# Prompt attention on one Trainium2 core: the last 16 keys of a query block turned onto higher partitions, and the value products of two units run together

## The chip, the cores and the metric

The kernel runs on one NeuronCore of a Trainium2 chip. A core has five engines that run side by side, each through its own instructions in order: TensorE (PE in the profile; its weight loads are listed apart as PEld), VectorE (DVE), ScalarE (ACT), GpSimd (POOL) and SyncE (SP, which here only issues DMAs). They meet through semaphores. The metric is the device time of one execution in microseconds: 2818.92 us, the median of three runs (2814.28 to 2822.15).

## The reference

One inference step of a two-layer decoder for a prompt of 1024 tokens (with 16 meta tokens ahead of it) and for eight short decode requests. The part that matters here is the attention of the prompt: 16 heads of 64, 1040 keys, causal, with a per-key log-forget sum `c` added to the scores.

```python
def one_block(args):
    qi, ci, pi = args
    s = jnp.einsum('bqhd,bkhd->bhqk', qi, k, preferred_element_type=f32)
    s = s + ci.astype(f32).transpose(0, 2, 1)[..., None] - ckT[:, :, None, :]
    s = jnp.where(pos_k[None, :] <= pi[:, None], s, -jnp.inf)
    p = jax.nn.softmax(s, axis=-1)
    return jnp.einsum('bhqk,bkhd->bqhd', p.astype(v.dtype), v)
```

The result is multiplied by a sigmoid gate, which the kernel has stored as `og2D`.

## The kernel before

The prompt attention is one stage, `attend_prompt` (L2707 on). It goes through 8 pairs of heads `hp` (two heads, `z` = 0 and 1, on partitions 0 to 63 and 64 to 127), and within a pair through four groups of two query blocks, in the order `QG = (0, 3, 1, 2)`. Query block `qb` = 2g+u+1 sees 16 + 128·qb keys, so there are 2g+1 or 2g+2 full tiles of 128 keys, and 16 keys more at the end. Those last 16 keys are the subject of the change; only the last 32 columns of queries of the block are taken for them.

**Scores** (`scores`, L2814). For each block the keys are cut into pieces (`KSPLIT`, 14 pieces for a pair). A piece is six matmuls (L2841): two heads by three products of high and low parts, into two PSUM tiles `sp`. There are three `sp` buffers in all. VectorE (L2845) adds the forget row `ncb` (or, for the diagonal 128 keys, `nd`, which GpSimd makes from `ncb` at L2811), takes the running maximum, and so frees the buffer. ScalarE takes the exponential (L2868).

**Units** (`units`, L2871). Two key tiles make a unit; a group has g+1 of them, and the last one, with `tail`, has one or two tiles and the 16 keys. `turn` turns the probabilities on TensorE: a 64 x 128 piece of the row `s` is the stationary operand and the identity the moving one (L2895), into the PSUM tile `tp` (two buffers). The tail turns its 16 keys by four ordinary float32 matmuls with 16 columns of `s` as weights (L2899; the profile counts two per float32 matmul), out to partitions 0 to 15. ScalarE copies `tp` to `th` (L2903) and the 16 rows to `tail` (L2905), a 128 x 128 tile that is zero elsewhere. `prod` multiplies with the values (L2928, L2932) and, for the 16 keys, `tail` with tile 2g+1+u of `vr`, whose first 16 rows are these keys (L2936); before that it spreads the reciprocal sums with four transposes (L2923). Products land in the PSUM tile `op`, of which there is one. VectorE then does three multiplications (L2939, L2942), and GpSimd splits the result (L2945, L2946).

**Order.** TensorE, VectorE, ScalarE and GpSimd take the order in which the code is written. The loop at the end of `attend_prompt` does for each unit: score pieces that are due (`ahead`), `turn`, exponentials, score pieces, and then `prod` of the unit before (`late`). The order on SP is not written; the framework places the DMAs there. SP issues the loads of the stage: for a pair, queries and keys `qh`, `kh`, `kl`, `ql` (L2760), the forget rows `ncb` (L2761), the values `vr` (L2767) with the 16 last keys apart into a ninth tile that GpSimd clears first (L2768, L2769), and the gates `og` (L2773). At the start of the stage the matmuls of the last gate tiles (`og`, L193 to L195) stand between the score pieces. The stage ahead of it is the attention of the decode requests, whose meta-token part ends in L2678, L2685 and L2691.

Of the kernel before, what the change touches and what calls it, by code (L numbers as in the profile page):

```python
# [8 lines left out]
F32 = mybir.dt.float32  # L9
# [8 lines left out]
P = 128  # L18
# [4 lines left out]
NM = 16  # L23
# [2683 lines left out]
def attend_prompt(self, ys):  # L2707
# [3 lines left out]
    with self.pool("ap", bufs=1) as sp, self.pool("ap2", bufs=2) as s2, self.pool("app", bufs=2, space=PSUM) as pp:  # L2711
# [41 lines left out]
        def place_c(hp):  # L2753
            return s2.tile([P, 2, NP], F32, name=f"ncb_{hp}", tag=f"ncb{hp % 2}", bufs=1)
# [116 lines left out]
        def units(hp, g):  # L2871
# [7 lines left out]
            out = []  # L2879
            for j0 in range(0, nf, 2):  # L2880
# [3 lines left out]
                def turn(j0=j0, tail=tail, hold=hold):  # L2884
                    pt = pp.tile([P, 2, 8, 64], F32, name=f"tp{hp}_{g}_{j0}", tag="tp")
                    th = s2.tile([P, 2, 2, 256], F32, name=f"th{hp}_{g}_{j0}", tag="th", bufs=3)
                    hold["th"] = th
# [4 lines left out]
                    for y, (z, u, j) in enumerate(ts):  # L2892
                        for h in range(2):
                            r = slice(h * 64, h * 64 + 64)
                            nc.tensor.transpose(pt[:, h, y], ss[z, u][r, j * P : j * P + P], self.ident[r, r])  # L2895
                    if tail:
                        for z in range(2):
                            for u in range(2):
                                nc.tensor.matmul(pt[:NM, 1, 6 + z, u * 32 : u * 32 + 32],  # L2899
                                                 ss[z, u][64:, (nf + u) * P : (nf + u) * P + NM],  # L2900
                                                 self.ident[64:, 96:], start=True, stop=True)
                    n = len(ts)
                    nc.scalar.copy(th.rearrange("p x z (u h q) -> p h (x z u) q", h=2, q=64)[:, :, :n], pt[:, :, :n])  # L2903
                    if tail:
                        nc.scalar.copy(tw[:NM], pt[:NM, 1, 6:].rearrange("p a q -> p (a q)"))  # L2905
                        hold["r"] = firstm.pop("r") if "r" in firstm else s2.tile([P, 2, 2], F32, name=f"r{hp}_{g}",
                                                                                  tag="r", bufs=4)
                        nc.vector.reciprocal(hold["r"], sm)
                        rx = hold["rx"] = firstm.pop("rx") if "rx" in firstm else s2.tile(
                            [P, 2, 2, DH], F32, name=f"rx{hp}_{g}", tag="rx")  # L2910
                        nc.gpsimd.tensor_copy(rx, hold["r"].unsqueeze(3).broadcast_to([P, 2, 2, DH]))

                def prod(j0=j0, tail=tail, hold=hold):
                    th = hold["th"]
                    mm = nc.tensor.matmul
                    if tail:


                        hold["rs"] = [hold["pt"][:, 0, 6:], po[:, 256:384].rearrange("p (u q) -> p u q", u=2)]
                        for u in range(2):  # L2920
                            for h, x in enumerate(hold["rs"]):
                                r = slice(h * 64, h * 64 + 64)
                                mm(x[:, u], hold["rx"][r, u].rearrange("p z d -> p (z d)"), self.ident[r, r],  # L2923
                                   start=(h == 0 or j0 == 0), stop=True, is_transpose=True, skip_group_check=True)
                    ds = [slice(z * 64, z * 64 + 64) for z in range(2)]
# [7 lines left out]
                    for u in range(2):  # L2933
                        for z in range(2):
                            c = (2 * z + u) * 32
                            mm(po[ds[z], u * P + 96 : u * P + P], vr[:, nf + u, ds[z]], tw[:, c : c + 32],  # L2936
                               start=False, stop=(u == 1))
# [9 lines left out]

                out.append((turn, prod))
            return out
# [12 lines left out]
        with tc.manual_schedule(engines={E.PE, E.DVE, E.Activation, E.Pool}):  # L2962
# [48 lines left out]
            late()  # L3011

# [33 lines left out]
```

## Time and profile before

| | |
|---|---|
| median of 3 runs | 2818.92 us |
| the profiled execution's own time (its span) | 2818.5 us |
| prompt attention, first score to last product | 1728.9 to about 1981 us |
| one pair of heads in the settled part | about 28.9 us (the piece of 400 columns after the first product run starts at 1818.63 and again at 1847.53) |
| busy in 1820 to 1880: PE, DVE, ACT, POOL | 56.78, 43.35, 45.56, 30.83 of 60 us |

How to read it: the profile is one execution. Its timeline lists an engine's instructions by start and duration, equal ones that follow each other as one row with their count, and in brackets the idle time before a row and what ended it. Two starts that follow each other tell how long the engine was held, which for matmuls is a better measure than the duration, since matmuls overlap. Semaphore waits are put down to the engine whose signal came last.

### The profile page before, as it was taken

The page shows a single profiled execution, that of the slowest core. Times are in us where ns is not written, and L with a number is a line of the kernel's source. Part 1 is how long each engine was busy: PE and PEld are TensorE (multiplying, and loading weights), DVE is VectorE, ACT ScalarE, POOL GpSimd, SP SyncE. Part 2 cuts the span into 40 slices and gives each one's busy share as a digit, 9 for nine tenths or more (in the row PEclk, how much of TensorE's full clock was granted, in tenths as well). Part 3 has the DMA queues.
Part 4 walks back from the last instruction along what each step waited for, and adds up shares of the span by engine and source line. Part 5 has one row for each costly group of instructions (what it writes and reads, how often), then busy time and mean ns, then how long its engine had stood idle before and what let it go on. Part 6 is the DMA issues. An engine that isn't in the chain of part 4 may idle for free. (4 is left out here: it accounts for less than half of the span.)

```text
span 2818.5 us, 60631 instructions
## 1 busy us (share of the span) xinstructions
PE 2762.3 (98%) x23543; PEld 2650.7 (94%) x23543; DVE 1798.8 (64%) x4025; ACT 1177.1 (42%) x2299; POOL 856.1 (30%) x1348
## 2 busy tenths in 40 slices
PE   9999989999999999999999999999999999999998
PEld 8998879999999999999999887677999999999998
DVE  5633566888887655662455444776388888766656
ACT  5432553422223334443444455777343223323345
POOL 3142333223223232124452202444313223323111
PEclk9999999999999999999999999999999999999999
DMA  7666555355564375544443775432524655527556
GB/s 213 174 188 170 151 164 193 108 152 158 173 178 137 120 246 171 192 145 163 145 173 123 264 293 193 161 128 87 157 87 126 177 176 163 162 91 236 179 195 215
DMA packets 432420, 474.05 MB, mean 168 GB/s; under 512 B 37015, under 2 KB 358291, under 8 KB 431107
## 3 DMA queue, kind: packets, MB, share of 16 engines
q1 hardware_dynamic: 380562, 320.52, 36.9%
q0 software_dynamic: 44928, 143.44, 15.5%
q10 hardware_dynamic: 6640, 6.21, 0.7%
q8 instruction: 185, 3.03, 0.5%
q14 instruction: 105, 0.85, 0.1%
HBM read 322.84 MB, written 147.21 MB: 167 GB/s over the span
## 5 line engine op out<-in xcount | busy, mean ns | idle before, releaser
L1614 PE MATMUL m<-xh,slot 128*128 128x276 f32 x2752 | 541.0, 290 | 1.8 <-ACT fs L1643 1.8
L1614 PEld LDWEIGHTS m<-xh,slot 128*128 128x128 f32 x2752 | 440.1, 188 | 3.6 <-ACT fs L1643 2.2
L1614 PE MATMUL m<-xl,slot 128*128 128x276 f32 x1376 | 397.3, 289 | 0.0
L1614 PEld LDWEIGHTS m<-xl,slot 128*128 128x128 f32 x1376 | 259.0, 188 | 0.0
L193 PE MATMUL tmps<-slot,xh 128*128 128x256 f32 (+2 forms) x864 | 243.1, 281 | 0.0
L195 PE MATMUL tmps<-slot,xl 128*128 128x256 f32 (+2 forms) x864 | 240.6, 278 | 0.0
L194 PE MATMUL tmps<-slot,xh 128*128 128x256 f32 (+2 forms) x864 | 240.5, 278 | 0.0
L272 DVE TENSOR_TENSOR slot<-slot,slot 128x1024 fp32r<-128x1024 f32 x124 | 162.9, 1314 | 60.1 <-ACT slot L271 58.7
L271 ACT CAST slot<-slot 128x1024 fp32r<-128x1024 f32 x124 | 129.5, 1045 | 142.6 <-PE m L1614 111.7
L194 PEld LDWEIGHTS tmps<-slot,xh 128*128 128x128 f32 (+1 forms) x864 | 159.1, 184 | 0.1
L195 PEld LDWEIGHTS tmps<-slot,xl 128*128 128x128 f32 (+1 forms) x864 | 158.6, 184 | 0.0
L193 PEld LDWEIGHTS tmps<-slot,xh 128*128 128x128 f32 (+1 forms) x864 | 158.4, 183 | 0.2
L193 PE MATMUL mmA<-xh,whi 128*128 128x384 f32 (+1 forms) x384 | 135.2, 352 | 0.1
L195 PE MATMUL mmA<-xh,wlo 128*128 128x384 f32 (+1 forms) x384 | 128.2, 334 | 0.0
L194 PE MATMUL mmA<-xl,whi 128*128 128x384 f32 (+1 forms) x384 | 128.1, 334 | 0.0
L272 DVE TENSOR_TENSOR slot<-vA,slot 128x1024 fp32r<-128x1024 f32 (+1 forms) x59 | 82.2, 1396 | 32.7 <-ACT slot L271 31.5
L272 DVE TENSOR_TENSOR slot<-Ht,slot 128x1024 fp32r<-128x1024 f32 (+1 forms) x59 | 81.4, 1382 | 32.2 <-ACT slot L271 31.1
L271 ACT CAST slot<-Ht 128x1024 fp32r<-128x1024 f32 (+1 forms) x59 | 61.0, 1036 | 96.8 <-PE m L1614 92.9
L271 ACT CAST slot<-vA 128x1024 fp32r<-128x1024 f32 (+1 forms) x59 | 60.8, 1035 | 95.5 <-PE m L1614 88.5
L1718 DVE TENSOR_TENSOR ws<-ws 128x128 f32<-128x128 f32 x264 | 93.8, 355 | 8.9
L2868 ACT ACTIVATE s<-s,nb 128x272 f32<-128x272 f32 (+7 forms) x126 | 98.8, 786 | 0.0
L2903 ACT COPY th<-tp 128x768 f32<-128x768 f32 (+1 forms) x80 | 73.6, 920 | 55.9 <-PE tp L2895 32.8
(809 smaller groups left out, 8688.7 us busy)
## 6 DMA issues: line engine op xcount, KB each, us to landing
ws<-in_w_down SPq DMA_DIRECT2D x176, 128.0 KB, 2.7
sD<-ws SPq DMA_DIRECT2D x176, 128.0 KB, 2.1
slot<-sD SPq DMA_DIRECT2D x40, 512.0 KB, 4.0
slot<-in_w_gate_up SPq DMA_DIRECT2D x36, 512.0 KB, 4.1
kp<-in_cache_k SPq DMA_DIRECT2D x32, 512.0 KB, 7.1
vp<-in_cache_v SPq DMA_DIRECT2D x32, 512.0 KB, 5.5
vA<-in_w_gate_up SPq DMA_DIRECT2D x26, 512.0 KB, 3.9
Ht<-in_w_gate_up SPq DMA_DIRECT2D x26, 512.0 KB, 3.9
```

Of the source, the lines that this page charges most:

```text
L193: mm(ps, sh, mh, start=first, stop=False)
L194: mm(ps, sh, ml, start=False, stop=False)
L195: mm(ps, sl, mh, start=False, stop=last)
L271: self.nc.scalar.copy(hi, src)
L272: self.nc.vector.tensor_tensor(out=lo, in0=src, in1=hi.bitcast(F32), op=ALU.subtract)
L1614: nc.tensor.matmul(u.ps[h, b], w[p][:, k], x[q][:, k], start=first and k == i == 0, stop=k == 3 and i == 2, skip_group_check=True)
L1718: tt(out=o, in0=a, in1=b, op=ALU.subtract)
L2868: nc.scalar.activation(ss[z, u], ss[z, u], AF.Exp, bias=nb[:, z : z + 1], accum_out=sm[:, u, z : z + 1])
L2903: nc.scalar.copy(th.rearrange("p x z (u h q) -> p h (x z u) q", h=2, q=64)[:, :, :n], pt[:, :, :n])
```

## The change

The last 16 keys are turned by weights of 80 columns (even pairs) or 112 columns (odd pairs) that end at these keys, so that they come out on partitions 64 to 79 or 96 to 111; columns ahead of them land on lower partitions of `tp` and are not read. Their values no longer lie in the first rows of the next `vr` tile but in a tile `vt` of their own, on the same partitions, one slot for each query block. `vt` is one tile for the whole stage, cleared once and loaded pair by pair. There are four `tail` tiles in place of two. The spread of the reciprocals is taken out of `prod` into `spread`. The products are held until two units wait, or until the last that waits is a group's tail; then `flush` runs the spreads and after them the products. A fourth `th` tile, `thx`, joins the three, and the four are used in turn.

```diff
-            nc.gpsimd.memset(vr[:, 8, :], 0.0)
-            e.dma_start(vr[:NM, 8, :], self.vD[8 * P :, cs])
+            e.dma_start(vt[at_tail(hp), :, :], self.vD[NM:, cs].rearrange("(j p) d -> p j d", p=P)[P - NM :])
...
+        vt = sp.tile([P, 8, P], F32, name="vt")
+        thx = sp.tile([P, 2, 2, 256], F32, name="thx")
+        tails += [sp.tile([P, P], F32, name=f"tail{x}") for x in (2, 3)]
+        for x in (vt, *tails[2:]):
+            nc.gpsimd.memset(x, 0.0)
+        at_tail = lambda hp: slice(64 + 32 * (hp % 2), 64 + 32 * (hp % 2) + NM)
+        ths = []
+
+        def place_t(nm):
+            if len(ths) < 4:
+                ths.append(thx if len(ths) == 3 else s2.tile([P, 2, 2, 256], F32, name=nm, tag="th", bufs=3))
+                return ths[-1]
+            ths.append(ths.pop(0))
+            return ths[-1]
...
-            tw = tails[QG.index(g) & 1]
+            tw = tails[2 * (hp % 2) + (QG.index(g) & 1)]
...
                     if tail:
+                        m = at_tail(hp).stop
                         for z in range(2):
                             for u in range(2):
-                                nc.tensor.matmul(pt[:NM, 1, 6 + z, u * 32 : u * 32 + 32],
-                                                 ss[z, u][64:, (nf + u) * P : (nf + u) * P + NM],
+                                e = (nf + u) * P + NM
+                                nc.tensor.matmul(pt[:m, 1, 6 + z, u * 32 : u * 32 + 32], ss[z, u][64:, e - m : e],
                                                  self.ident[64:, 96:], start=True, stop=True)
...
-                        nc.scalar.copy(tw[:NM], pt[:NM, 1, 6:].rearrange("p a q -> p (a q)"))
+                        nc.scalar.copy(tw[at_tail(hp)], pt[at_tail(hp), 1, 6:].rearrange("p a q -> p (a q)"))
...
+                def spread(hold=hold):
+                    hold["rs"] = [hold["pt"][:, 0, 6:], po[:, 256:384].rearrange("p (u q) -> p u q", u=2)]
+                    for u in range(2):
+                        for h, x in enumerate(hold["rs"]):
+                            r = slice(h * 64, h * 64 + 64)
+                            nc.tensor.matmul(x[:, u], hold["rx"][r, u].rearrange("p z d -> p (z d)"), self.ident[r, r],
+                                             start=(h == 0 or not begun), stop=True, is_transpose=True,
+                                             skip_group_check=True)
...
-                            mm(po[ds[z], u * P + 96 : u * P + P], vr[:, nf + u, ds[z]], tw[:, c : c + 32],
+                            mm(po[ds[z], u * P + 96 : u * P + P], vt[:, nf + u - 1, ds[z]], tw[:, c : c + 32],
                                start=False, stop=(u == 1))
...
-            late = None
+            late = []
+
+            def flush():
+                for z in (2, 1):
+                    for x in late:
+                        if x[z]:
+                            x[z]()
+                late.clear()
+
...
-                    if late:
-                        late()
-                    late = us[k][1]
+                    if len(late) == 2 or (late and late[-1][2]):
+                        flush()
+                    late.append(us[k])
```

What stands where on the engines. First SP at the start of the stage, before (the names are DMA targets and sources; the semaphores of the waits are named by engine, DMAHW and DMASW being DMA queues):

```order
L2661 DMA vmS<-vD 16x1024 [waits DMAHW5_49,DMASW1_49,PE_49]
L2760 DMA qh_20709<-qDh 128x1040 [waits DMAHW6_49]
L2760 DMA kh_20716<-kDh 128x1040 [waits DMAHW7_49,Activation_49]
L2760 DMA kl_20717<-kDl 128x1040 [waits DMAHW0_49]
L2760 DMA ql_20718<-qDl 128x1040 [waits DMAHW1_49]
L2761 DMA ncb_20721<-cD 128x2080 [waits DMAHW2_49]
L2767 DMA vr_20688<-vD 128x8x128 [waits DMAHW3_49,DVE_49]
L2769 DMA vr_20688<-vD 16x128 [waits DMAHW4_49,Pool_49]
```

And the same place of the changed kernel (line numbers from 2768 on are its own):

```order
L2661 DMA vmS<-vD 16x1024 [waits DMAHW5_49,DMASW1_49,PE_49]
L2768 DMA vt<-vD 16x8x128 [waits DMAHW6_49,DVE_49,Pool_49]
L2760 DMA qh_20709<-qDh 128x1040 [waits DMAHW7_49,Activation_49]
L2760 DMA kh_20716<-kDh 128x1040 [waits DMAHW0_49]
L2760 DMA kl_20717<-kDl 128x1040 [waits DMAHW1_49]
L2760 DMA ql_20718<-qDl 128x1040 [waits DMAHW2_49]
L2761 DMA ncb_20721<-cD 128x2080 [waits DMAHW3_49,PE_49]
L2767 DMA vr_20688<-vD 128x8x128 [waits DMAHW4_49]
```

The load of `vt`, which waits for GpSimd, now stands ahead of the five loads that the first scores need; before, the load that waits for GpSimd stood behind them. What GpSimd has there in the changed kernel (`mneg` is the causal mask, `sM` a softmax row of the decode stage, `nd` the masked forget rows):

```order
L2720 MEMSET tail_20683 128x128
L2715 AFFINE_SELECT mneg<-mneg 128x128 [waits Pool_49]
L2720 MEMSET tail_20684 128x128
L2805 MEMSET vt 128x1024 [waits DMAHW4_49,DMAHW2_49,DMAHW5_49,DMAHW1_49,PE_49]
L2805 MEMSET tail_20724 128x128
L2805 MEMSET tail_20725 128x128
L2425 TENSOR_TENSOR sM_20626<-sM_20626,nb_20647 128x16 [waits DVE_49]
```

The three L2805 rows are new. The clearing of `vt` waits for a TensorE count that is reached with the second run of L2678, the meta-token scores of the decode stage.

Second, TensorE in the first product runs of a long group (`hp` = 2, g = 3), before; `sp_6_0` and `sp_6_1` are two score pieces that belong to a later group, `tp_3_4` the turn of unit 2, `op` the products of unit 0:

```order
L2841 MATMUL sp_6_0_0_22245<-kh_21265,ql_21267 128x400
L2841 MATMUL sp_6_0_1_22246<-kh_21265,ql_21267 128x400
L2928 MATMUL op_3_22165<-th_3_0_22167,vr_21726 64x256 x4
L2841 MATMUL sp_6_1_0_22259<-kh_21265,qh_21264 128x384
L2841 MATMUL sp_6_1_1_22260<-kh_21265,qh_21264 128x384
```

Unit 1's products followed in the same way behind the turn of unit 2. In the changed kernel the two score pieces touch, and the products of units 0 and 1 follow the turn as one run:

```order
L2854 MATMUL sp_6_0_0_22229<-kh_21263,ql_21265 128x400
L2854 MATMUL sp_6_0_1_22230<-kh_21263,ql_21265 128x400
L2854 MATMUL sp_6_1_0_22239<-kh_21263,qh_21262 128x384
L2854 MATMUL sp_6_1_1_22240<-kh_21263,qh_21262 128x384
L2854 MATMUL sp_6_1_0_22239<-kl_21264,qh_21262 128x384
```

and behind the rest of the second piece and the first four turns of unit 2:

```order
L2908 MATMUL tp_3_4_22254<-ident,s_7_0_21836 128x64 x2
L2908 MATMUL tp_3_4_22254<-ident,s_8_0_21910 128x64 x2
L2908 MATMUL tp_3_4_22254<-ident,s_7_1_21837 128x64 x2
L2908 MATMUL tp_3_4_22254<-ident,s_8_1_21911 128x64 x2
L2943 MATMUL op_3_22151<-th_3_0_21033,vr_21720 64x256 x4
L2943 MATMUL op_3_22151<-th_3_2_21088,vr_21720 64x256 x4
```

Counted over the stage, the product runs (a run being all products with no turn or score between them) go from 80 to 48; 32 of them begin with a spread, before and after.

More of the change, by code (lines that the diff above doesn't have):

```diff
@@ L2875, in units @@
             ss, sm = rows[hp, g]
-            tw = tails[QG.index(g) & 1]
+            tw = tails[2 * (hp % 2) + (QG.index(g) & 1)]
             po = pp.tile([P, 512], F32, name=f"op{hp}_{g}", tag="op", bufs=1)
             nf = 2 * g + 1
-            out = []
+            out, begun = [], []
             for j0 in range(0, nf, 2):
@@ L2885, in turn @@
                     pt = pp.tile([P, 2, 8, 64], F32, name=f"tp{hp}_{g}_{j0}", tag="tp")
-                    th = s2.tile([P, 2, 2, 256], F32, name=f"th{hp}_{g}_{j0}", tag="th", bufs=3)
+                    th = place_t(f"th{hp}_{g}_{j0}")
                     hold["th"] = th
@@ L2915, in prod @@
                     mm = nc.tensor.matmul
[L2916 to L2924, printed above, removed]
+                    begun.append(j0)
                     ds = [slice(z * 64, z * 64 + 64) for z in range(2)]
@@ L2946, in prod @@
                     nc.gpsimd.tensor_tensor(out=xl, in0=y, in1=xh.bitcast(F32), op=ALU.subtract)
-                out.append((turn, prod))
+                out.append((turn, prod, spread if tail else None))
             return out
@@ L3010, in attend_prompt @@
                     next(tile0)
-            late()
+            flush()
 _INS = ["x_prompt", "x_sample", "state_C", "state_n", "state_m", "cache_k", "cache_v", "cache_logf", "page_table",
```

## The prediction

> **What bounds the kernel now.** I read the page first, then the busy times of the settled part of the stage, then who waits for whom there, and then the timeline where the order changes.
>
> ```profile
> span 2818.5 us, 60631 instructions
> PE 2762.3 (98%) x23543; PEld 2650.7 (94%) x23543; DVE 1798.8 (64%) x4025; ACT 1177.1 (42%) x2299; POOL 856.1 (30%) x1348
> 1820.00:1880.00 60.00, 56.78 (x809) 42.74 (x807) 43.35 (x215) 45.56 (x98) 30.83 (x76) 1.00 0.44 146
>   issue: 15.4, 35
>   DVE mx L2845: 10.9, 26
> ```
>
> The second row gives the busy times of the engines, the third the window 1820 to 1880: TensorE 56.78 of 60 us, VectorE 43.35, then ScalarE and GpSimd. So TensorE sets the pace, and a microsecond taken from it counts, unless it only moves into a wait. The last two rows are what the score matmuls (L2841) waited for: 10.9 us in all for VectorE, which frees the three `sp` buffers, and 15.4 us put down to no one. TensorE has some 3 us of such waits in a pair of 28.9 us; the order decides how many.
>
> **The start of the stage.** The load of `vt` now heads SP's queue and waits for GpSimd's clearing, which waits for the second run of L2678. These are SP's issues, the kilobytes and landing time of this `ncb` and the least, median and longest of all eight, GpSimd, TensorE and VectorE there:
>
> ```profile
> 1715.09 0.42 SPq L2760 DMA_DIRECT2D qh<-qDh  x1
> 1716.98 0.46 SPq L2761 DMA_DIRECT2D ncb<-cD  x1
> ncb<-cD SPq DMA_DIRECT2D x1, 1040.0 KB, 10.5
> DMA to landing us min/median/max: 7.9/7.9/10.5
> 1717.34 0.53 POOL L2671 MEMSET qmt<- 128x512 f32 x1 [9.34 <-PE mps L2678]
> 1723.78 0.22 POOL L2720 MEMSET tail<- 128x128 f32 x1
> 1727.00 0.22 POOL L2425 TENSOR_TENSOR sM<-sM,nb 128x16 f32<-128x16 f32 x1 [3.00 <-DVE nb L2422]
> 1729.56 2.80 POOL L2811 TENSOR_TENSOR nd<-ncb,mneg 128x256 f32<-128x256 f32 x4
> 1723.40 1.06 PE L2678 MATMUL mps<-ktS,qmt 128*128 128x16 f32 x8
> 1731.47 0.59 PE L2841 MATMUL sp<-kh,qh 64*128 64x272 f32 x2
> 1729.52 0.17 DVE L2845 CUSTOM_DVE_ANT_0 s<-sp,ncb 128x16 f32<-128x16 f32 x1
> 1730.34 0.35 DVE L2845 CUSTOM_DVE_ANT_0 s<-sp,nd,mxf 128x128 f32<-128x128 f32 x1 [0.64 <-POOL nd L2811]
> ```
>
> L2678 ends at 1723.40 + 1.06 = 1724.46. A clearing of 512 columns took 0.53 and of 128 took 0.22, so 1024 take about 0.94: until 1725.4. With 0.1 for the signal and about 0.4 for issuing `vt`, `qh` goes out at 1725.9 where it went at 1715.1: 10.8 us later. The earliest place of the clearing is behind the memset of 1723.78, half a microsecond sooner; the latest is ahead of `sM` at 1727.00, which stands behind it. `ncb` comes 1.9 us behind `qh` and took 10.5 us to land, since four loads are ahead of it: 1716.98 + 10.5 + 10.8 = 1738.3. Before, it was there at 1727.5 and first used at 1729.5, so 2 us of slack are eaten first. Then GpSimd makes `nd` (0.73, a quarter of 2.80), VectorE needs 0.4, and at 1739.5 the second matmul of the piece of 272 columns gets its buffer, where it started at 1731.47: **+8.0 us**. Nothing covers it, because TensorE runs in order and the gate matmuls stand between the pieces. The bounds are 5.5 (`ncb` landing in 7.9, the median) and 12 (a slower landing, and a spell of half clock after the idle time).
>
> **The turned tail.** The rows of TensorE from one stretch of pair 2, with two of L364 for weights of 92 columns, a score that waits behind a tail, two of a tail's products and four of the stretch behind; at the end two starts on VectorE:
>
> ```profile
> 1818.12 0.71 PE L2895 MATMUL tp<-ident,s 64*128 64x64 f32 x16
> 1818.63 0.42 PE L2841 MATMUL sp<-kh,qh 64*128 64x400 f32 x2
> 1819.59 1.08 PE L2928 MATMUL op<-th,vr 128*64 128x256 f32 x8 [0.17 <-PE sp L2841]
> 1820.61 0.44 PE L2841 MATMUL sp<-kh,qh 64*128 64x384 f32 x2
> 1821.23 0.66 PE L2895 MATMUL tp<-ident,s 64*128 64x64 f32 x16
> 1821.82 1.08 PE L2928 MATMUL op<-th,vr 128*64 128x256 f32 x8
> 1822.83 0.34 PE L2841 MATMUL sp<-kh,qh 64*128 64x144 f32 x2
> 1823.23 0.55 PE L2895 MATMUL tp<-ident,s 64*128 64x64 f32 x12
> 1823.70 0.40 PE L2899 MATMUL tp<-ident,s 64*16 64x32 f32 x8
> 1824.04 0.68 PE L2841 MATMUL sp<-kh,qh 64*128 64x272 f32 x2
> 447.06 1.06 PE L364 MATMUL nps<-ones,sq 128*92 128x1 f32 x12
> 447.99 0.37 PE L193 MATMUL pops<-xh,wo 128*128 128x276 f32 x1
> 1830.83 0.41 PE L2841 MATMUL sp<-kh,qh 64*128 64x384 f32 x1 [0.51 <-DVE mx L2845]
> 1834.37 0.39 PE L2932 MATMUL op<-th,vr 128*64 128x128 f32 x4
> 1834.58 0.38 PE L2936 MATMUL op<-tail,vr 128*64 128x32 f32 x8
> 1834.89 0.40 PE L2841 MATMUL sp<-kh,qh 64*128 64x272 f32 x2
> 1835.37 0.66 PE L2895 MATMUL tp<-ident,s 64*128 64x64 f32 x16
> 1837.18 0.45 PE L2841 MATMUL sp<-kh,qh 64*128 64x400 f32 x2
> 1837.84 0.53 PE L2895 MATMUL tp<-ident,s 64*128 64x64 f32 x12
> 1820.06 0.57 DVE L2845 CUSTOM_DVE_ANT_0 s<-sp,ncb 128x400 f32<-128x400 f32 x1
> 1836.73 0.36 DVE L2845 CUSTOM_DVE_ANT_0 s<-sp,ncb,mx 128x144 f32<-128x144 f32 x1
> ```
>
> Eight L2899 matmuls held TensorE for 1824.04 − 1823.70 = 0.34, and the 12 turns ahead of them for 0.47, where 16 turns ahead of a score take 0.51, so 12 should take 0.38: changing to the small shape costs 0.09, and a like amount sits in the 0.34. The new shape, 64 x 128, is that of the turns and scores, and both go. But the weights grow from 16 to 80 or 112 columns. L364 has weights of 92 columns and one moving column, and takes (447.99 − 447.06)/12 = 0.078 each, so a column of float32 weights costs 0.85 ns when nothing longer hides it. That makes 0.068 and 0.095 for one, 0.54 and 0.76 for eight. Net: 0.54 − 0.34 − 0.09 = +0.11 in even pairs, +0.33 in odd ones; 16 of each: **+7.0 us of TensorE work**. Unseen is whether such weights load beside the matmul ahead on the same 64 rows. Fully hidden, eight cost at most 0.34 less 0.09 for the exit, and a tail saves 0.18: −5.8 us. Not hidden at all, with 0.04 more for each matmul, +17. I stay at the cadence of L364, the nearest in columns.
>
> [...]
>
> **The merged products.** Eight L2928 hold TensorE for 1.01 (1821.82 to 1822.83). Four L2932 of half their columns hold it for 0.21, so eight L2928 stream in 0.84 to 0.88, and about 0.13 is the change of shape behind a run. Ahead of a run the 16 turns take 0.59 instead of 0.51: 0.08. A run that is merged away saves 0.2; there are 32 fewer: **−6.4 us of TensorE work**. With the tails that is +0.6, or nothing. So the waits decide.
>
> The waits come from the three `sp` buffers. Before, a product run lay between two score pieces and VectorE emptied a buffer under it. Stretch one, pieces of 400 and 384: in the old order 1818.63 to 1822.83 is 4.20. In the new one the piece of 384 follows at once, and its second matmul needs the buffer that VectorE leaves at 1820.06 (it works off the multiplications of the group before first). So it starts at 1820.13, the piece takes another 0.60, the turns 0.59, 16 products 0.88 + 1.01 = 1.89, and the next piece comes at 1823.21: **+0.38** in place of a saving. Stretch two, from the 272 at 1834.89: the piece of 400 now comes 0.97 later, behind 16 turns, and needs the buffer that VectorE leaves 1.84 after that start (1836.73); it ends at about +2.5 with a run of 0.88 still owed, where it ended at 1837.84, +2.95, with that run done: +0.43, of which the shorter next wait gives 0.2 back: **+0.23**. The two stretches between (512 and 384 after a turn) lose 0.4 and 0.55 in such waits and get most of it back from the wait that a 384 has behind a tail now (0.51 idle at 1830.83, and as much under the first matmul): +0.1. In these three the longer tails are counted; three of the four tails of a pair stand ahead of a score that waits anyway. The fourth, the next pair's first, does not: +0.11 or +0.33, mean **+0.22**. A pair: +0.93; seven pairs **+6.5 us**. In the last pair no scores are left: three fewer runs −0.6, three tails of 112 columns +1.0, and a wait of 0.6 for the one `op` buffer goes: −0.2. The bounds for all this are +0.6 (no more waits than now) and +13 (twice mine, since each wait is read off one row).
>
> **What hides.** The later loads of `vt` wait for the products of a pair's first group only and are first read behind the second, longest group, so they cost nothing unless SP is late by a group. The eight clearings on `vr` go from GpSimd, which is half idle. A copy of 16 rows from other partitions is not in the trace; ScalarE has 14 us idle in 60, which covers it. The fourth `th` lets no turn wait: a buffer is read at least two units before it is written again.
>
> **The sum.** 2818.5 + 8.0 + 6.5 − 0.2 = 2832.8 in the profiled execution, whose span lies 0.4 under the median: **2833 us**.
>
> **Rivals.** (A) The clock. After a window in which TensorE was busy 2.67 of 3.40 us, the granted clock (the number behind the engines) was at half in the next:
>
> ```profile
> 1795.20:1798.60 3.40, 2.67 (x39) 1.99 (x35) 3.28 (x10) 2.92 (x10) 0.53 (x2) 1.00 0.89 286
> 1798.60:1802.00 3.40, 2.84 (x13) 1.58 (x13) 2.27 (x11) 0.63 (x2) 2.15 (x5) 0.50 0.38 134
> ```
>
> Two waits of 0.9 and 0.4 in one such stretch would make it as idle. A stretch of 3.4 at half clock costs up to 1.7; one in each pair gives 2846. Against it: 1820 to 1880 ran at 1.00 with waits of 0.5 to 0.9 in it. [...] (B) The start alone: VectorE's waits are absorbed, leaving 8.0 + 0.6: 2827. For it: VectorE has 28% idle. (C) The start is hidden, because `ncb` lands sooner without the stores of the gate tiles beside it, and the settled part costs 6.5: 2825. (D) TensorE pays mostly for changes of shape: weights load hidden, tails save 5.8 and runs 6.4, no new waits: 2818.5 + 8 − 12 = 2814.5. It decides in favour of the change once the start costs less than these 12 us; with a start of 4 or less it is 2810 or faster. For it: the 0.09 around the small shape is plainly there. Against it: 0.078 a matmul in L364, with one moving column and 92 of weights, and 0.042 (0.34/8) in L2899 with 32 moving and 16 of weights. [...]
>
> **Chances.** Forecast 0.45 (2828 to 2840), A 0.20, B 0.17, C 0.07, D 0.11. The range leaves out half of D below and the worst of A above: 2816 to 2850. A measurement of this kernel tells 0.3% (8.5 us) from no change: slower by more are the forecast, A and half of B, 0.73; faster by more is D with a short start, 0.05; within 0.3% the rest, 0.22.
>
> **What would show it.** `qh` issued about 10 us later and TensorE idle some 7 us between the first two pieces; eight tail matmuls holding TensorE for 0.54 and 0.76; a run of 16 products in 1.9; the piece of 384 waiting 0.9 behind the 400; a pair of 29.8 us. I am wrong if the tails hold TensorE no longer than now, if the pair is shorter than 28.9, or if `ncb` is there when the first score ends.

## The result and the profile after

| | before | changed |
|---|---|---|
| median | 2817.88 us (4 runs, 2814.28 to 2822.15) | 2840.56 us (4 runs, 2836.23 to 2843.71) |
| ratio | | 1.0080, 95% interval 1.0068 to 1.0091 |
| the profiled execution's span | 2818.5 us | 2842.1 us |

The change makes the kernel 0.8% slower. Forecast were 2833 us, with a range of 2816 to 2850: the sign and the range hold, the size was 14 us and is 23.

The head of the page of the changed kernel, the same window of its settled part (columns as before), and what its score matmuls, now L2854, waited for in the whole stage:

```profile
span 2842.1 us, 60620 instructions
PE 2768.0 (97%) x23543; PEld 2666.7 (94%) x23543; DVE 1800.3 (63%) x4025; ACT 1184.3 (42%) x2299; POOL 855.6 (30%) x1343
...
1820.00:1880.00 60.00, 55.01 (x776) 44.62 (x776) 42.16 (x208) 45.40 (x93) 28.90 (x72) 1.00 0.42 146
...
  DVE mx L2858: 28.2, 53
  PE tp L2908: 10.8, 14
  issue: 8.4, 15
```

The number to see is the first of the last three. The scores waited for VectorE 26 times and 10.9 us in all; now it is 53 times and 28.2 us. (The view counts matmuls and their weight loads; for the matmuls alone it is 16 waits of 6.8 us in all, and now 35 of 17.5.) TensorE is busy for 55.01 of 60 us where it was for 56.78, and the window holds fewer of its matmuls (776 for 809). In this window only the weight loads take more time (44.62 us for 42.74); TensorE waits more.

The start of the stage, TensorE and then SP. The second run of L2678, which stood at 1723.40 before, is the mark to measure from, because TensorE's code and order are the same up to there:

```profile
1726.03 1.06 PE L2678 MATMUL mps<-ktS,qmt 128*128 128x16 f32 x8
...
1733.87 0.33 PE L2854 MATMUL sp<-kh,qh 64*128 64x144 f32 x2 [2.24 <-DMA kh<-kDh]
1735.47 0.49 PE L2854 MATMUL sp<-kl,qh 64*128 64x144 f32 x2 [1.27 <-DMA kl<-kDl]
1737.03 0.49 PE L2854 MATMUL sp<-kh,ql 64*128 64x144 f32 x2 [1.07 <-DMA ql<-qDl]
...
1742.22 0.56 PE L2854 MATMUL sp<-kh,qh 64*128 64x272 f32 x1 [1.36 <-DVE mxf L2858]
...
1728.56 0.38 SPq L2760 DMA_DIRECT2D qh<-qDh  x1
...
1730.47 0.44 SPq L2761 DMA_DIRECT2D ncb<-cD  x1
```

`qh` goes out 2.53 us behind the mark, where it went 8.31 us ahead of it: 10.84 later. The second matmul of the 272 columns starts 16.19 behind the mark, where the piece started 8.07 behind it: +8.1. The waits for `kh`, `kl` and `ql`, all inside the first piece, take 4.6 us, and that for VectorE (which had no `ncb`) 1.4.

The clock fell among these waits, at 1734.9, behind a window (1731.5 to 1734.9) in which TensorE was busy for 0.46 of 3.40 us. Three windows of the start; the number behind the five engines is the granted clock:

```profile
1734.90:1738.30 3.40, 1.76 (x7) 1.43 (x8) 0.00 (x0) 0.00 (x0) 0.00 (x0) 0.50 0.85 331
1738.30:1748.50 10.20, 8.84 (x32) 6.84 (x31) 3.09 (x19) 2.19 (x5) 4.85 (x10) 0.50 1.03 379
1748.50:1751.90 3.40, 3.40 (x21) 2.88 (x21) 1.74 (x8) 2.62 (x3) 0.58 (x1) 1.00 1.01 363
```

Half clock lasts for 13.6 us, where before it lasted for 3.4 at this place, so that the first group ends 9.6 us later than before, not 8.1.

The settled part, the two stretches of the pair `hp` = 2 on which the prediction rested (TensorE):

```profile
1831.44 0.44 PE L2854 MATMUL sp<-kh,qh 64*128 64x400 f32 x2
...
1832.08 0.34 PE L2854 MATMUL sp<-kh,qh 64*128 64x384 f32 x1
1833.03 0.44 PE L2854 MATMUL sp<-kh,qh 64*128 64x384 f32 x1 [0.61 <-DVE mx L2858]
...
1834.23 1.95 PE L2943 MATMUL op<-th,vr 128*64 128x256 f32 x16
1836.11 0.33 PE L2854 MATMUL sp<-kh,qh 64*128 64x144 f32 x2
...
1843.13 0.49 PE L2914 MATMUL tp<-ident,s 64*80 64x32 f32 x5
1843.40 0.44 PE L2854 MATMUL sp<-kh,qh 64*128 64x384 f32 x1
1843.46 0.38 PE L2914 MATMUL tp<-ident,s 64*80 64x32 f32 x3
...
1848.41 0.39 PE L2854 MATMUL sp<-kh,qh 64*128 64x272 f32 x2
...
1849.36 0.42 PE L2854 MATMUL sp<-kh,qh 64*128 64x400 f32 x1
1850.48 0.42 PE L2854 MATMUL sp<-kh,qh 64*128 64x400 f32 x1 [0.70 <-DVE mx L2858]
...
1854.77 0.59 PE L2908 MATMUL tp<-ident,s 64*128 64x64 f32 x12
```

The 384 now touches the 400, and its second matmul comes 0.95 us behind the first (1832.08, 1833.03), because VectorE has not emptied a buffer. 400 to 144 takes 4.67 us where it took 4.20. From the 272 of stretch two to the turn of the tail unit behind the second pair of products it takes 6.36 (1848.41 to 1854.77); before, that turn stood here:

```profile
1840.80 0.59 PE L2895 MATMUL tp<-ident,s 64*128 64x64 f32 x12
```

which is 5.91 behind 1834.89. A pair takes 30.25 us and 30.04 us in turn, where it took 28.87.

### The profile page after: what moved, and what is told of

Its sections match the earlier page's. It is cut to its first block, busy times and chain, and to the rows that moved or that the text cites. A ratio compares the mean times of both kernels' runs of the same rounds, so it can differ in the third digit from the quotient of the medians.

```text
span 2842.1 us, 60620 instructions
## 1 busy us (share of the span) xinstructions
PE 2768.0 (97%) x23543; PEld 2666.7 (94%) x23543; DVE 1800.3 (63%) x4025; ACT 1184.3 (42%) x2299; POOL 855.6 (30%) x1343
## 5 line engine op out<-in xcount | busy, mean ns | idle before, releaser
L195 PE MATMUL tmps<-slot,xl 128*128 128x256 f32 (+2 forms) x864 | 240.6, 278 | 0.0
L195 PEld LDWEIGHTS tmps<-slot,xl 128*128 128x128 f32 (+1 forms) x864 | 158.6, 184 | 0.0
L195 PE MATMUL mmA<-xh,wlo 128*128 128x384 f32 (+1 forms) x384 | 127.5, 332 | 0.0
L272 DVE TENSOR_TENSOR slot<-vA,slot 128x1024 fp32r<-128x1024 f32 (+1 forms) x59 | 82.2, 1396 | 32.7 <-ACT slot L271 31.5
L2292 DVE TENSOR_REDUCE ss<-sqb 128x4 f32<-128x256 f32 (+1 forms) x72 | 30.2, 419 | 100.1 <-ACT sqb L2291 99.5
```

The costliest lines, as they stand in the source:

```text
L195: mm(ps, sl, mh, start=False, stop=last)
L272: self.nc.vector.tensor_tensor(out=lo, in0=src, in1=hi.bitcast(F32), op=ALU.subtract)
L2292: nc.vector.tensor_reduce(out=ss[:m, i, :], in_=sq[:m].rearrange("p (h d) -> p h d", d=DH), op=ALU.add, axis=AX.X)
```

## The experiments

The table has every run. "First group" is the time from the second run of L2678 to the last L2936 (or its line there) of the first group, "pairs" the time of even and odd pairs (by `hp`) in the settled part (from the last L2936 of one pair to that of the next), "last" the eighth pair, "behind" the time from there to the end of TensorE's work. They are worked out from the traces; a settled pair with a spell of half clock in it is left out, and so are one or two in e1, e3, e6, e9 and e12 that take 0.2 to 0.4 us longer than their like. Each ratio is against executions of the kernel before in the same session (medians of 2815.4 to 2818.1 us). Where no ratio stands, there was one execution.

| run | median us | ratio, 95% interval | first group | pairs, even / odd | last | behind |
|---|---|---|---|---|---|---|
| before | 2817.9 | | 32.2 | 28.88 / 28.86 | 22.5 | 829.3 |
| changed | 2840.6 | 1.0080 (1.0068, 1.0091) | 41.8 | 30.25 / 30.04 | 26.4 | 827.7 |
| e1 unit by unit | 2828.7 | 1.0046 (1.0029, 1.0063) | 41.9 | 29.07 / 28.90 | 24.2 | 827.3 |
| e2 merging alone | 2833.7 | 1.0058 (1.0040, 1.0076) | 31.0 | 30.05 / 30.05 | 23.2 | 835.3 |
| e3 vt on another queue | 2835.4 | 1.0061 (1.0045, 1.0078) | 36.3 | 30.28 / 30.03 | 24.7 | 827.2 |
| e4 and new tiles behind | 2841.3 | 1.0080 (1.0063, 1.0096) | 33.2 | 30.24 / 30.07 | 26.4 | 835.6 |
| e5 light VectorE | 2808.3 | | 30.8 | 27.63 / 27.63 | 21.9 | 826.6 |
| e6 light, merged | 2812.7 | | 30.6 | 28.53 / 28.53 | 22.6 | 825.1 |
| e7 tails alone | 2819.3 | 1.0010 (1.0000, 1.0020) | 30.5 | 29.07 / 28.87 | 25.7 | 826.7 |
| e8 VectorE relieved | 2827.2 | 1.0041 (1.0025, 1.0056) | 32.2 | 29.26 / 29.37 | 23.4 | 833.7 |
| e9 sp unread | 2812.9 | | 30.7 | 28.45 / 28.45 | 22.8 | 826.0 |
| e10 sp unread, merged | 2819.2 | | 30.6 | 28.93 / 29.44 | 22.1 | 825.1 |
| e11 pieces moved | 2818.3 | 1.0006 (0.9997, 1.0015) | 31.9 | 28.70 / 28.70 | 23.6 | 826.7 |
| e12 no stall | 2831.6 | 1.0053 (1.0037, 1.0068) | 30.5 | 30.27 / 30.06 | 24.7 | 827.6 |

**Which part costs in the settled pairs.** e1 undoes the merging and keeps the rest of the change:

```diff
-                    if len(late) == 2 or (late and late[-1][2]):
+                    if late:
```

> The changed kernel, but the products of each unit run as soon as the next unit is turned, as before the change (80 runs of products, not 48); new tails and start stay. The settled pairs of the changed kernel take 30.03 and 30.25 us in turn (28.87 before). Theory (the merging costs through waits for the sp buffers, three of a pair's four tails are hidden): pairs of 29.0 to 29.2, waits at the scores back to those of before, 2831 us. Rival 1 (the wider weights are what costs, all four tails bare): pairs of 29.3 (80 columns) and 30.2 (112), 2836. Rival 2 (shape changes are what TensorE pays for, the merging is a gain of 0.8 a pair): pairs of 30.8 or more, 2846.

e2 does the merging alone. Against the changed kernel:

```diff
-            e.dma_start(vt[at_tail(hp), :, :], self.vD[NM:, cs].rearrange("(j p) d -> p j d", p=P)[P - NM :])
+            nc.gpsimd.memset(vr[:, 8, :], 0.0)
+            e.dma_start(vr[:NM, 8, :], self.vD[8 * P :, cs])
...
-                                nc.tensor.matmul(pt[:m, 1, 6 + z, u * 32 : u * 32 + 32], ss[z, u][64:, e - m : e],
+                                nc.tensor.matmul(pt[:NM, 1, 6 + z, u * 32 : u * 32 + 32],
+                                                 ss[z, u][64:, (nf + u) * P : (nf + u) * P + NM],
...
-        thx = sp.tile([P, 2, 2, 256], F32, name="thx")
+        thx = s3.tile([P, 2, 2, 256], F32, name="thx")
```

> The merged runs and the fourth th alone: tail of 16 columns and its values in the ninth tile of vr as before, the new tiles placed behind all others so that nothing else moves in memory; the start as before. Theory (waits for sp): a pair takes 29.8 to 30.0 us, the 384 behind the 400 waits about 0.9, 2828 us. Rival (the merging saves 0.8 of TensorE work a pair and its waits are absorbed): 28.1, 2812.

The waits of TensorE in two settled pairs, first before, then the changed kernel, e1 and e2 (engine, line, what it waited for: us in total, times, the longest):

```profile
PE sp L2841 <- DVE mx L2845: 1.5, 4, 0.5
```

```profile
PE sp L2854 <- DVE mx L2858: 4.2, 9, 0.7
```

```profile
PE sp L2854 <- DVE mx L2858: 1.4, 3, 0.7
```

```profile
PE sp L2854 <- DVE mx L2858: 3.9, 8, 0.7
```

Unit by unit the waits are those of before (1.4 us); with the merging alone they are those of the change (3.9). A pair costs 1.18 us more in e2 and 0.04 to 0.19 more in e1, and the two add up to about the 1.17 and 1.38 of the change. So the tails are nearly hidden, and the merging is the loss. The windows over the same two pairs, before and e2:

```profile
1875.72:1933.46 57.74, 54.52 (x786) 41.07 (x780) 42.06 (x209) 43.66 (x93) 29.40 (x74) 1.00 0.43 149
```

```profile
1875.00:1935.09 60.09, 54.78 (x778) 42.80 (x777) 42.30 (x209) 43.95 (x94) 29.32 (x74) 1.00 0.44 144
```

TensorE's idle time grows from 3.22 to 5.31 us, by 1.04 in a pair: most of the 1.18. e2's total came out at 2833.7, not 2828, for a reason of the experiment's own: its new tiles lie behind all others, as it seems on memory that the first weights of the next stage (`slot`) used before. Their load goes out at 1989.26, just behind the last products, where before ScalarE cast them at 1979.80 already. The first matmul of that stage waits for them:

```profile
1994.42 0.60 PE L532 MATMUL pops<-xh,slot 128*128 128x276 f32 x1 [5.24 <-ACT slot L271]
```

Its column "behind" has 835.3 for 829.3, and e4, with the same placement, 835.6.

**What stalls the start.** e3 takes the load of `vt` from the head of SP's queue:

```diff
-            e.dma_start(vt[at_tail(hp), :, :], self.vD[NM:, cs].rearrange("(j p) d -> p j d", p=P)[P - NM :])
+            (e if hp else nc.gpsimd).dma_start(vt[at_tail(hp), :, :], self.vD[NM:, cs].rearrange("(j p) d -> p j d", p=P)[P - NM :])
```

> The changed kernel, but the first load of vt goes out on GpSimd's queue, so that nothing stands ahead of qh on SP. Theory of the prediction (this load is the whole stall of the start): the stall of about 9.6 us is gone, 2831. Rival (a second wait lies under it: the new tiles push ncb onto memory that the last matmuls of the decode gate still read, so that the load of ncb waits for L195, which ends 3.8 us behind the start of the second run of L2678): qh, kh, kl and ql go out 10 us sooner, ncb at most 0.7 us sooner; the second score piece still waits for ncb and some 3 to 6 us of the stall stay, 2835.

The timeline of e3, the mark, then SP, then the second score piece:

```profile
1727.37 1.07 PE L2678 MATMUL mps<-ktS,qmt 128*128 128x16 f32 x8
...
1719.14 0.36 SPq L2760 DMA_DIRECT2D qh<-qDh  x1
...
1731.17 0.32 SPq L2761 DMA_DIRECT2D ncb<-cD  x1
...
1739.27 0.36 PE L2854 MATMUL sp<-kh,qh 64*128 64x272 f32 x1 [3.92 <-DVE mxf L2858]
```

`qh` goes out 8.23 us ahead of the mark, as before. `ncb` goes out 3.80 behind it, 0.64 sooner than in the changed kernel, and the second piece still waits 3.92 us. The second wait is real: in SP's waits of e3 the load of `ncb` stands with 10.2 us for `bps` at L195. The new tiles push `ncb` onto memory that these last gate matmuls ahead of the stage still read. Of the 9.6 us, 4.1 are left. e4 also puts the new tiles behind all others (`s3` is a pool opened behind `s2`):

```diff
-    with self.pool("ap", bufs=1) as sp, self.pool("ap2", bufs=2) as s2, self.pool("app", bufs=2, space=PSUM) as pp:
+    with self.pool("ap", bufs=1) as sp, self.pool("ap2", bufs=2) as s2, \
+            self.pool("ap3", bufs=1) as s3, self.pool("app", bufs=2, space=PSUM) as pp:
...
-        vt = sp.tile([P, 8, P], F32, name="vt")
-        thx = sp.tile([P, 2, 2, 256], F32, name="thx")
-        tails += [sp.tile([P, P], F32, name=f"tail{x}") for x in (2, 3)]
+        vt = s3.tile([P, 8, P], F32, name="vt")
+        thx = s3.tile([P, 2, 2, 256], F32, name="thx")
+        tails += [s3.tile([P, P], F32, name=f"tail{x}") for x in (2, 3)]
```

> The same, and the new tiles placed behind all others, so that ncb lies where it lay before the change. Both theories: qh and ncb go out as before, TensorE does not wait between the first pieces, the first group ends 9 to 10 us sooner than in the changed kernel against the second run of L2678, 2831. The settled pairs stay at 30.03 and 30.25. If a stall of over 2 us is left, a third cause is at work (the clearing of vt, GpSimd's order).

The first group ends 0.95 us behind that of before, but the kernel is no faster: the 8 us are paid back behind the stage, as in e2. e12 reaches the same without that, by creating the tile of `ncb` (and `kh`, `kl`, `ql`) ahead of the rows of blocks 1, 2 and 8:

```diff
-        first[0] = [place_k(0, "qh")]
+        first[0] = [place_k(0, nm) for nm in ("qh", "kh", "kl", "ql")]
+        firstc[0] = place_c(0)
...
-        first[0] += [place_k(0, nm) for nm in ("kh", "kl", "ql")]
...
-        firstc[0] = place_c(0)
```

with e3's edit beside it.

> The changed kernel with both causes at the start taken away without moving anything behind the stage: the first load of vt on GpSimd's queue, and the tile of ncb placed ahead of the rows of blocks 1, 2 and 8. Theory: the first group ends within 2 us of before, pairs of 30.03 and 30.25, last pair 2.2 us longer than before where the clock stays up; 2829 to 2832 us, 9 to 11 less than the changed kernel. Rival (something else at the start): 2835 or more.

It does what was expected: 2831.6 us, and no wait at the start. e7 is this and e1's edit together, so that of the change the new tails (and `thx`) are left:

> Of the change only the tails of 80 and 112 columns with vt (and thx): products unit by unit, the first load of vt on GpSimd's queue, and the tile of ncb placed ahead of the rows of blocks 1, 2 and 8, so that it lies on no memory that the decode gate still reads. Theory: no stall at the start (first group's end within 1 us of before), pairs of 28.9 and 29.1 as in e1, last pair 1.7 us longer: 2821 us, no difference that can be told from before. Rival (a third cause at the start): 2825 or more.

2819.3 us, 1.0010 (1.0000 to 1.0020): the tails cannot be told from before. That hides a little: e7's first group is 1.7 us shorter than that of before, whose profiled execution had a spell of half clock there; without one the same first group takes 30.7 to 30.8 us (e5 and e9, whose first pair is unchanged). By e1's pairs the tails cost about 2.5 us, some 0.1 in each of seven pairs and 1.7 in the last.

**Whether the waits are VectorE's.** e5 and e6 put VectorE's score operation on half of each piece's columns from the second pair on, in the order of before and in the merged one (with the old tail, as in e2). So that the other half has old values to keep, the rows `s` also stay in one buffer each, where two took turns:

```diff
-                    ss[z, u] = firsts.pop((qb, z)) if (qb, z) in firsts else row(hp, qb, z)
+                    ss[z, u] = firsts[qb, z]
...
                         for y, (o, e) in enumerate(parts):
+                            e = e if hp == 0 else (o + e) // 2
...
-                                in1=diag[x][:, z] if y else ncb[:, z, at + o : at + e], scale=1.0,
+                                in1=diag[x][:, z, : e - o] if y else ncb[:, z, at + o : at + e], scale=1.0,
```

> The kernel before, with VectorE's score operation on half of each piece's columns from the second pair on (the other half of a row keeps what the pair before left; the output is not the reference's). TensorE's work and order stay. With e6 it asks what merging costs when the sp buffers come free sooner. Both theories: pairs shorter than 28.87, 26.5 to 28, since some 2.7 us of a pair are waits for these buffers.

> The merged runs and the fourth th with the old tail, as in e2, and the same half score operation from the second pair on; ncb is placed ahead of the rows of blocks 1, 2 and 8, so that nothing waits at the start. Theory (the merging costs only through the sp buffers): its pairs are shorter than those of e5_light_before, by 0.4 to 0.8 us. Rival (it costs through something else, such as the copies of ScalarE or the single op buffer): longer than those by about 1.2, as e2 is against before.

The first came as expected (27.63). The second did not: the merged order still costs 0.90 us a pair (0.2 to 0.3 more in two of its pairs), nearer to the rival's 1.2 than to a gain. What TensorE waits for decides between the two. The waits of e6 in 60 us:

```profile
PE sp L2852 <- DVE mx L2857: 2.6, 6, 0.9
PE tp L2907 <- DVE og L2955: 0.6, 2, 0.3
```

In e5 the same window has no wait for `mx` at all. So the cost is still a wait for `sp`, but half the columns don't remove it: a piece that touches the next has to wait at least for the first operation on it. At 1845.94 VectorE, idle just before, starts on a piece of 400; the second matmul of the 384 behind it comes at 1846.37, 0.73 us behind the first. The theory stands, the size that I expected of this test does not.

e9 and e10 take the wait for `sp` away altogether: from the second pair on VectorE reads the forget row in its place.

```diff
-                                out=ss[z, u][:, at + o : at + e], in0=ps[z][:, o:e],
+                                out=ss[z, u][:, at + o : at + e], in0=ncb[:, z, at + o : at + e] if hp else ps[z][:, o:e],
```

> The kernel before, but from the second pair on VectorE's score operation reads the forget row where it read the PSUM tile sp (the scores of pairs 2 to 8 are computed and read by no one; the output is not the reference's). TensorE's instructions and their order stay, and no score matmul has to wait for VectorE any more. Both theories: no wait of a score for VectorE in the settled part, pairs of 26 to 27.5 us.

> The merged runs and the fourth th with the old tail, as in e2, and the same score operation that reads no sp from the second pair on. Theory (the price of merging, 1.18 us a pair, is waits for sp): most of the price is gone; the pairs are at most 0.5 us longer than in e9, or shorter, down to the 0.6 that the products save. What is left of it must then stand in the waits of the spreads for GpSimd's reciprocals, which lose the cover of a product run too. Rival (a cost of the merged order that is no wait for sp): pairs longer than in e9 by 0.9 to 1.2.

This pair is inconclusive on the size. No score waits for VectorE any more in either, but e9's pairs are 28.45, longer than expected, because VectorE's operation got slower (last section). The merged order costs 0.48 and 0.99 us in the two pairs of e10 that ran at full clock. In e10 this stands in both of these pairs, and in e9 at the place of the first (second fence):

```profile
PE tp L2929 <- POOL rx L2922: 2.7, 2, 1.9
```

```profile
PE op L2928 <- DVE og L2942: 1.0, 1, 1.0
PE tp L2923 <- POOL rx L2911: 0.7, 1, 0.7
```

With the waits for `sp` gone, the merged order shows another: the spreads wait for GpSimd's reciprocals, 2.7 us for 0.7. The run of products had covered that chain too.

**Two tries for a faster kernel.** e8 leaves the order of before and takes the three multiplications behind a group from VectorE:

```diff
-                    nc.vector.tensor_tensor(out=y, in0=po[:, :256], in1=y, op=ALU.mult)
+                    w = s2.tile([P, 2, 256], F32, name=f"ev{hp}_{g}", tag="ev", bufs=1)
+                    nc.scalar.copy(w[:, 0], po[:, :256])
...
+                    nc.gpsimd.tensor_tensor(out=y, in0=w[:, 0], in1=y, op=ALU.mult)
```

> The kernel before, with the three multiplications behind a group's products taken from VectorE: ScalarE copies the products and the spread reciprocals out of PSUM (three copies), GpSimd multiplies. Theory (VectorE's release of the sp buffers sets the waits): pairs of 28.0 to 28.6, 2812 to 2816 us, faster than both kernels. Rival (the op buffer and ScalarE's queue become the wait): pairs of 29.2 or more, 2822 or slower.

The rival came. The waits of two pairs:

```profile
PE tp L2895 <- ACT ev L2942: 1.2, 2, 0.6
PE tp L2923 <- POOL rx L2911: 0.9, 2, 0.5
PE op L2928 <- ACT ev L2941: 0.9, 4, 0.3
PE sp L2841 <- DVE mx L2845: 0.4, 2, 0.2
```

The waits for `sp` fall from 1.5 to 0.4 as they should. In their place come 2.1 us of waits for ScalarE's copies, where 1.1 us went to VectorE's multiplications before, and 0.9 for GpSimd's reciprocals, where there were none. With the tile `ev` the first matmul of the next stage also waits, 7.50 us for `slot`. e11 moves score pieces, nothing else:

```diff
-KSPLIT = {1: (144,), 2: (272,), 3: (400,), 4: (272, 256), 5: (400, 256), 6: (400, 384), 7: (512, 400),
-          8: (384, 384, 272)}
+KSPLIT = {1: (144,), 2: (272,), 3: (400,), 4: (272, 256), 5: (256, 400), 6: (512, 272), 7: (512, 400), 8: (384, 384, 272)}
...
-LEAD = 9
+LEAD = 8.2
```

> The kernel before with its score pieces in other places, and nothing else: LEAD 8.2 for 9, block 5 cut as 256 and 400 for 400 and 256, block 6 as 512 and 272 for 400 and 384. The same work, placed so that a run of products stands between more of the pieces. Theory (what stands between two pieces decides): the waits of scores for VectorE fall from the 0.75 us a pair of before to under 0.3, pairs of 27.7 to 28.3, 2810 to 2814 us, faster than both kernels. Rival (the waits only move to other places): pairs of 28.8 or more, 2818.

A pair is 0.17 us shorter, and the last pair gives 1 us back: 1.0006 (0.9997 to 1.0015), no difference. No version that computes the whole result beat the kernel before.

## Why the prediction was right in sign and short in size

The profiled execution is 23.6 us longer. 2.6 of it lie ahead of the mark and −1.6 behind the stage, in code that did not change; the stage itself has 22.6. The prediction's sum was 14.3:

| term | predicted | measured | how measured |
|---|---|---|---|
| start | +8.0 | +9.6 | end of the first group |
| the rest of the first pair and six more pairs | +6.5 | +8.7 | 1.1 in the first, then 1.16 to 1.40 each at full clock |
| last pair | −0.2 | +2.25 | 24.7 in e3 and e12, at full clock, against 22.5 |
| half clock in the rest of the stage | 0 | +2.0 | 2.4, 2.0 and 1.6 in three pairs, less 4.0 that before had in one; of the 2.4 and of the 4.0 (both `hp` = 1) some 1.5 are no clock, since e1, e3 and e7 take 30.4 to 31.5 there at full clock |

**The start** was right in its place and time (10.84 for 10.8, the second matmul +8.1 for +8.0). The clearing took 0.95, `vt` went out 0.03 behind its end and `qh` 0.42 behind `vt`, where 0.94, 0.1 and 0.4 were taken; the 0.1 for the signal was an estimate that no row showed. Its cause was told by half. The step "The load of `vt` now heads SP's queue and waits for GpSimd's clearing" is true and worth 5.5 us (e3). Under it lay the wait of `ncb` for the gate matmuls. It can be read in the order printed above, where `ncb` has "PE_49" among its waits and had not before; the prediction passed over it. Two causes that end at about the same time hide each other: taking away one alone gives only what it adds to the other (here 5.5 us in e3, and 11.3 with both taken away in e12). "Nothing covers it" holds, and the idle time cost more than itself: 1.5 us more were lost behind it, where half clock went on, which the bound of 12 had room for and the value had not. The 9.6 are measured against an execution that had 3.4 us of half clock there itself; against the 30.7 and 30.8 of e5 and e9, whose first pair is that of before at full clock, the start cost 11.1. "TensorE idle some 7 us between the first two pieces" was misplaced: 4.6 of the 5.9 us lie inside the first piece, which waits for `kh`, `kl` and `ql`; the prediction had no such wait. The end came out the same because `ncb` lands last.

**The tail.** The weights' columns cost what L364 said: behind the first, whose gap is shorter, the eight matmuls of a tail start 0.072 us apart with 80 columns and 0.098 to 0.099 with 112 (starts in the trace), where 0.068 and 0.095 were taken. In the last pair, where no score follows, eight hold TensorE for 0.85 us:

```profile
2002.57 0.92 PE L2914 MATMUL tp<-ident,s 64*112 64x32 f32 x8
...
2003.42 1.95 PE L2943 MATMUL op<-th,vr 128*64 128x256 f32 x16
```

The 0.09 for the change to the small shape went, as assumed, ahead of three of the four tails of the pair `hp` = 2: the 12 turns there take 0.38, 0.36 and 0.43, where they took 0.47, 0.46 and 0.52; ahead of the third they take 0.52 for 0.46. That three of the four tails hide was right. The fourth costs 0.02 and 0.2 (e1, e7), not 0.11 and 0.33, probably because the next score slips in between: in the pair `hp` = 2 one starts at 1855.57, between the fifth and the sixth matmul of such a tail of 112 columns. Rival D, shape changes as the price, falls with this.

**The merged products.** A run of 16 holds TensorE for 1.88 (1834.23 to 1836.11), 1.89 was worked out. All the saving is there, and all of it goes into waits, as forecast. The waits are what was sized too small: stretch one +0.47 for +0.38, stretch two +0.45 for +0.23, the rest of a pair 0.25 to 0.5 for 0.32. Both were read off one row, and the bound of twice the value covers it. One reading was off too: "some 3 us of such waits in a pair" spreads the view of the whole stage, start included, over the pairs. In the settled pairs TensorE waited 0.75 us a pair for VectorE at its scores.

**The last pair** is the step that failed: "a wait of 0.6 for the one `op` buffer goes: −0.2". The changed kernel has there

```profile
1991.62 0.24 PE L2932 MATMUL tp<-ident,rx 64*128 64x64 f32 x1 [0.79 <-ACT tail L2919]
...
1997.22 0.24 PE L2932 MATMUL tp<-ident,rx 64*128 64x64 f32 x1 [0.78 <-ACT tail L2919]
```

Before, a run of products stood between the turn of a tail and the spread, and ScalarE copied under it. The prediction asked of the merging only what it does to the `sp` buffers; the spread needs the copy of the tail, and lost its cover as well. Three tails have no score behind them; the one at 2002.57 adds 0.42 (0.85 less 0.33 less the 0.1 of the entry: the 12 turns ahead take 0.43, 2002.14 to 2002.57, where they took 0.52, 1977.93 to 1978.45). By parts, at full clock: the merging alone makes this pair 0.7 us longer (e2, 23.2), where the prediction made it 1.2 shorter; the tails alone make it 1.7 longer (e1, 24.2), where the prediction had 1.0. Three times 0.42 is 1.3; the rest of the tails' share stays open.

**The clock.** Rival A is true in part: the spells exist and cost 2.0 us net in this execution, but none lies in the settled pairs (`hp` = 2 to 5). B falls with e2, whose pairs take 30.05 us; C with the start itself, +9.6; D with e2 and e7, neither of which is faster than before.

## What to carry to other kernels

A merged run was cheaper by itself (16 products in 1.88 us, where two runs of eight took 1.02 and 1.01) and dear in waits (a pair 1.18 us longer in e2): what a run covered (a buffer that another engine empties, a copy, a chain of reciprocals) has to be listed for every run that is merged away, not only for the one resource that is known to be tight. A new tile was not free even where there was room: it moved other tiles onto memory with other last readers (`ncb` waited 10.2 us for L195 in e3, the next stage 5.24 for `slot` in e2), so the waits of each early load should be compared before and after. When two delays end at nearly the same time, undo both before judging either.

## What the runs showed that was not expected

A score matmul starts inside a tail's run, in 29 of the 32 tails. At 1843.40 one on the other 64 rows stands between five and three tail matmuls, although the code has it behind all eight; with 16 columns, before, no score starts until all eight have started, in any of the 32 (1823.70 and 1824.04).

Half clock followed windows of very different idle time: at the start one in which TensorE was busy for 0.46 of 3.40 us, in the last pair one with 2.35:

```profile
1990.90:1994.30 3.40, 2.21 (x28) 1.63 (x28) 0.42 (x1) 3.33 (x7) 0.00 (x0) 1.00 0.02 5
1994.30:1997.70 3.40, 2.35 (x42) 2.18 (x44) 0.58 (x4) 1.88 (x4) 1.48 (x3) 1.00 0.00 0
1997.70:2001.10 3.40, 3.40 (x26) 2.24 (x26) 0.00 (x0) 0.41 (x1) 0.00 (x0) 0.50 0.00 0
```

The busy share of the window ahead does not tell it by itself: the one ahead of the 2.35 was emptier (2.21) and was followed by full clock. What decides stays open.

VectorE's score operation took longer in part of its executions in e9, where it reads two SBUF operands in place of PSUM and SBUF. Here is one group of it, before and in e9 (duration in ns: least, median, longest; all of one size):

```profile
L2845 DVE CUSTOM_DVE_ANT_0 s<-sp,nd,mx x126: 349/351/353, 1733.0 to 1967.2; 128x128 f32<-128x128 f32 x126
```

```profile
L2845 DVE CUSTOM_DVE_ANT_0 s<-ncb,nd,mx x112: 350/352/898, 1760.9 to 1963.0; 128x128 f32<-128x128 f32 x112
```

The median is the same, the longest goes from 353 to 898 ns. All 32 that took over 400 ns ran beside an L2811 on GpSimd. The longest L2811 goes from 748 to 1042 ns as well. So the experiment that took away a read of PSUM changed more than a wait.
